# Hybrid encoder block: page names of the embedding stage, the order of the gate stage's end, the last root on ScalarE, rows stored weighted

## The chip, the cores and the metric

One core of a Trainium2 chip runs the whole program. The metric is the device time of one execution in microseconds; the time before is the median of three runs. A profiled execution, which the hardware profiler recorded, has its own time and a span, from its first to its last instruction.

## The reference

One encoder layer on 512 tokens of width 2048, all in float32:

```python
h = rms_norm(x, norm_mix_w);  proj = h @ w_in          # attention + gated linear attention
x = x + concat([y_a, y_g]) @ w_out
h = rms_norm(x, norm_ffn_w)
u = causal_depthwise_conv(h @ w_ffn_up, w_ffn_conv, b_ffn_conv)
x = x + (gelu(u_gate) * u_val) @ w_ffn_down
h = rms_norm(x, norm_ple_w)
g = sigmoid(h @ w_ple_gate)
x = x + g * (p @ w_ple_proj)
return rms_norm(x, final_norm_w)
```

The change touches the last four lines and nothing that is computed: `p @ w_ple_proj` (the embedding product), the gate `g`, its product and sum, and the last norm.

## The kernel before

Everything is held transposed: 128 channels on the partitions, 512 tokens along the row. A "unit" is a pair of channel blocks (m and m + 8), so that a unit's rows form a tile of 128 x 2 x 512 (1024 elements a partition). Large matrix products go by a Strassen-like scheme with seven products (P1 to P7) of quarter size a unit; their results are summed into four quarters: C11 and C21 hold tokens 0 to 255 (`lo`), C12 and C22 tokens 256 to 511 (`hi`), the first index is the block of the pair. Each product splits its float32 operand into a high and a low part (`wsplit`, or `last` for three products of the last pair that have tiles of their own): ScalarE copies the high part, VectorE subtracts. A product is 24 matmuls of 128x256. `prep` makes the split two products ahead, `collect` takes a product from its PSUM bank into `unit.o` (tile `u`), on ScalarE where it is a quarter's first part and on VectorE where it is added to one.

The work is a list `steps` of (unit, product). `agenda[i]` holds what is done beside step i, with a key: 0 ahead of all, 1 before the product, larger keys behind it. VectorE, ScalarE and TensorE keep this program order (`InOrder`); DMA issues do not unless they are marked with `tc.keep_in_program_order`, and a planner puts them where it sees fit on the queue of the engine that issues them (SP, ScalarE or GpSimd).

Weights come into nine pages (r0 to r8) which go round: `issue` loads the next wanted operand when a page is released, operands named L from SP, sums S from SP and GpSimd.

The embedding stage lies between the attention and the output projection. It has four units; each makes four 128x512 results by six matmuls each, which ScalarE copies in pairs into a page (tile `pp_o`) and stores from its own queue to `ppd` in memory. So eight pages are filled and stored; their names come from `PP_PAGES`. The names are those of pages that other stages use: c0 to c2 for residual rows `xs`, u0 to u3 for `unit.o`.

The gate stage (`pg`) is the last: eight units, of which the last two (u6, u7) go side by side in the order P1, P2, P6, P7, P4, P5, P3 (`HALVES`), the last fourteen steps. For units 0 to 5 `after_gate` multiplies `unit.o` by the norm's row `rb`, takes the sigmoid, multiplies by the embedding rows `ppl`, adds to the residual row `xs`, stores `xs` to `x3d` and sums its squares into `acc`. For the last pair the same is done by halves: `times_norm` (norm and sigmoid) and `add_gated` (product, sum, and the squares into a page of their own, `q`). Meanwhile `reload` brings back the rows of units 0 to 5 from `x3d` into tiles `x`, and `weigh` multiplies them by the final norm's column weights; `weigh_part` does so for the last two units.

The end, from the last four products on, is written out by hand. `sum_squares` makes the mean square on TensorE (tile `ms`), put between the matmuls of P3 for the low half and behind the last product for the high half. `root_begin` and `root_end` make the reciprocal root (tile `root`), with one Newton step: before, VectorE scales and adds, ScalarE takes the square root, VectorE the reciprocal. `finish` multiplies rows of a half by the root, a unit at a time (128x512), and stores the 256 KB piece; there are sixteen, eight low and eight high.

Of the kernel before, what the change touches and what calls it, by code (L numbers as in the profile page):

```python
# [16 lines left out]
D = 2048  # L17
# [26 lines left out]
def encoder_block(ctx: ExitStack, tc: tile.TileContext, A, out):  # L44
# [345 lines left out]
    def issue():  # L390
        kept, i = 0, 0
        while i < len(wanted):
# [11 lines left out]
            if name[0] == "L":  # L404
                nc.sync.dma_start(t, src(name))
            else:
                nc.sync.dma_start(t, src("L21"))
                nc.gpsimd.dma_start(t, src("L22" if name == "S1" else "L11"), accum_op=ALU.add)  # L408
# [283 lines left out]
    def after_gate(unit):  # L692
# [5 lines left out]
                (3, 0, lambda: nc.sync.dma_start(x3d[unit.u], xs))] + squares(unit, 2)  # L698
# [26 lines left out]
    def embedding(unit):  # L725

        hi, lo = unit.w["PP"]
        for i in range(4):
            if i % 2 == 0:
                tag = PP_PAGES[(2 * unit.u + i // 2) % 3]  # L730
# [368 lines left out]
    PP_PAGES = ("c2", "u1", "c1")  # L1099
# [94 lines left out]
    def reload(i):  # L1194
        t = xtile(("R11", "R21")[i // 2], i % 2, "x3", F32)
        for j in range(2):
            m = 2 * i + j
            if m < 6:
                x3[m] = t[:, j, :].rearrange("p (s t) -> p s t", s=2)
                nc.sync.dma_start(x3[m], x3d[m])  # L1200

    def weigh(m):
        for s in range(2):
            act.activation(x3[m][:, s, :], x3[m][:, s, :], AF.Copy, scale=nfin[:, m + 8 * s:m + 8 * s + 1])
# [14 lines left out]
    def add_gated(unit, s, c):  # L1219
        o, xs = unit.o[:, s, c], unit.xs[:, s, c]  # L1220
        vec.tensor_tensor(o, o, unit.pp[:, s, c], ALU.mult)
        vec.tensor_tensor(xs, xs, o, ALU.add)
        if unit not in sq_page:
            sq_page[unit] = spare("q").rearrange("p (s t) -> p s t", s=2)
        act.activation(sq_page[unit][:, s, c], xs, AF.Square)

    end = len(steps) - 14
    for n in range(2):
        agenda[end + 2].append((0, lambda n=n: reload(n)))
    agenda[end + 7].append((0, lambda: reload(2)))  # L1230
    for m in range(4):
        agenda[end + 5 + m].append((2, lambda m=m: weigh(m)))
# [122 lines left out]
    for i, (unit, prod) in enumerate(steps[:-4]):  # L1355
# [17 lines left out]
        if i == len(steps) - 5:  # L1373
            add_gated(units[-2], both, lo_half)
        if i - len(steps) in EARLY:
            p, op, g = EARLY[i - len(steps)]
            t = xtile(op, g, "last")
            prep(len(steps) + p, (t[:, 0, :], t[:, 1, :]))
        collect(unit, prod)
        if st.chained and st is not wo and unit.head is not None and i == base[unit] + 11:  # L1380
            norm_root()
        if st is stages[-1] and unit.last is not None:
            if prod == "P4" and unit is units[-2]:
# [18 lines left out]
    def root_begin(ms):  # L1402
        w = spare("root").rearrange("p (q t) -> p q t", q=4)
        vec.tensor_scalar(w[:, 0], ms, 1.0 / D, EPS, ALU.mult, ALU.add)
        act.activation(w[:, 1], w[:, 0], AF.Sqrt)
        return w

    def root_end(w):
        a, y, t, r = (w[:, q] for q in range(4))
        vec.reciprocal(y, y)  # L1410
# [5 lines left out]
    def finish(c, r, ms):  # L1416
        for m in ms:
            t = x3[m][:, :, c]
            vec.tensor_tensor(t, t, r[:, None, :].broadcast_to([P, 2, 256]), ALU.mult)
            (nc.sync if m % 2 else nc.scalar).dma_start(out2[m][:, :, c], t)  # L1420
# [13 lines left out]
    times_norm(u7, both, lo)  # L1434
    for s in range(2):
        vec.tensor_tensor(acc[:, lo], acc[:, lo], sq(u6, s, lo), ALU.add)
    add_gated(u7, both, lo)
    collect(u6, "P5")
    product(u7, "P5")
    times_norm(u6, 1, hi)  # L1440
    weigh_part(u6, range(2), lo)
    add_gated(u6, 1, hi)
    collect(u7, "P5")
    ms = {}
# [92 lines left out]
```

## Time and profile before

| | us |
|---|---|
| median of three runs (lowest, highest) | 2245.37 (2245.11, 2250.11) |
| profiled execution, its own time | 2245.14 |
| span of the profiled execution | 2242.8 |
| mean granted TensorE clock | 0.994 |
| gate stage's last pair, first product | starts at 2174.2 |
| last product ends | 2220.4 |
| VectorE's last row done | 2238.1 |
| embedding products | 597.7 to 626.4 |

How to read the lines: times are microseconds from the span's start; PE is TensorE's matmul, PEld its weight load, DVE VectorE, ACT ScalarE, POOL GpSimd, SP the engine that issues most DMAs. A name with q (SPq, ACTq) is that engine's queue issuing a DMA. A timeline line has start, duration, engine, source line, operation, out<-in, shapes and count; brackets hold the idle time before it and who ended it. Most lines show L64, the helper that records every operation, so the tile names tell them apart. A wait for several semaphores is put down to the one that came last.

### The profile page before, as it was taken

To read this page: it belongs to the slowest core of one execution; us is meant where nothing else is said; L and a number is where in the kernel's file an instruction comes from. 1 tells how busy PE (TensorE), PEld (TensorE's weight loads), DVE (VectorE), ACT (ScalarE), POOL (GpSimd) and SP (SyncE) were. 2 spreads that over 40 slices of the span, in tenths; PEclk is the share of its full clock that TensorE was granted. 3 is DMA by queue.
4 is the path that set the end of the run, shared out by engine and by line. 5 is a ranking of instruction groups with operands and counts; after the bars stand their busy time and mean duration, and the time that the engine had idled before them with its cause. 6 is when DMAs were issued, how large, how long until landed. Compare 5 with 4: busy or idle time off the path is not lost.

```text
span 2242.8 us, 46265 instructions
## 1 busy us (share of the span) xinstructions
PE 2196.2 (98%) x18588; PEld 2145.4 (96%) x18588; DVE 1927.1 (86%) x2636; ACT 1339.5 (60%) x2001; POOL 158.7 (7%) x196
## 2 busy tenths in 40 slices
PE   9999999999999999999999999999999999999996
PEld 7899999999889999999999999999999999999995
DVE  8476777999778888999888898889898887999997
ACT  9455565777665665555555555555564554667655
POOL 0000000000000100000000000010000100000000
PEclk9999999999999999999999999999999999999997
DMA  7476865667888987888888888888876968879994
GB/s 237 137 185 186 222 202 156 186 186 195 289 251 263 329 239 205 217 231 212 225 211 226 217 221 216 221 215 224 257 238 236 314 219 270 295 255 336 273 301 148
DMA packets 190759, 518.29 MB, mean 231 GB/s; under 512 B 20272, under 2 KB 66608, under 8 KB 190544
## 3 DMA queue, kind: packets, MB, share of 16 engines
q1 hardware_dynamic: 160272, 415.72, 54.9%
q0 software_dynamic: 25920, 93.33, 23.3%
q10 hardware_dynamic: 4352, 6.29, 0.8%
q8 instruction: 145, 2.38, 0.4%
q14 instruction: 70, 0.57, 0.1%
HBM read 441.86 MB, written 71.30 MB: 229 GB/s over the span
## 4 chain that ended last, share of the span: by engine, by line
PE 79%; DVE 10%; DMA 5%; ACT 4%; issue 2%; SPq 0%; ACTq 0%; DVEq 0%; POOLq 0%
PE accA L64 41%; PE accC L64 21%; PE accB L64 10%; DVE wsplit L64 3%; DMA l<-in_w_ple_gate 1%; DMA s<-in_w_v_a 1%; DVE u L64 1%; DVE l L64 1%; PE py L64 1%; PE ptr L64 1%; DMA ppd<-pp_o 1%; ACT wsplit L64 1%; PE psc L64 1%; PE v L243 1%; PE v L244 1%
## 5 line engine op out<-in xcount | busy, mean ns | idle before, releaser
L64 DVE TENSOR_TENSOR wsplit<-l,wsplit 128x1024 fp32r<-128x1024 f32 (+1 forms) x478 | 573.6, 1201 | 117.0 <-ACT wsplit L64 116.2
L64 ACT ACTIVATE wsplit<-l 128x1024 fp32r<-128x1024 f32 (+1 forms) x478 | 497.8, 1042 | 290.3 <-PE accC L64 121.0
L64 DVE TENSOR_TENSOR wsplit<-s,wsplit 128x1024 fp32r<-128x1024 f32 (+1 forms) x251 | 301.1, 1201 | 66.1 <-ACT wsplit L64 65.7
L64 ACT ACTIVATE wsplit<-s 128x1024 fp32r<-128x1024 f32 (+1 forms) x251 | 260.8, 1039 | 61.3 <-PE accB L64 37.4
L64 ACT ACTIVATE u<-accA 128x256 f32<-128x256 f32 x302 | 114.2, 378 | 272.3 <-PE accA L64 267.1
L64 PE MATMUL accA<-up_T,wsplit 128*128 128x256 f32 x2112 | 253.6, 276 | 0.4 <-ACT wsplit L64 0.4
L64 PEld LDWEIGHTS accA<-up_T,wsplit 128*128 128x128 f32 x2112 | 245.8, 188 | 0.7 <-ACT wsplit L64 0.6
L64 DVE SCALAR_TENSOR_TENSOR cv<-u,cw,cv 128x511 f32<-128x511 f32 (+1 forms) x176 | 131.6, 748 | 3.1
L408 POOL DMA_DIRECT2D s<-in_w_up x88 | 76.3, 867 | 764.3 <-DMA s<-in_w_up 416.4
L64 PE MATMUL accA<-up_N,wsplit 128*128 128x256 f32 x1056 | 127.1, 276 | 1.2 <-DVE wsplit L64 1.2
L64 PE MATMUL accA<-dn_T,wsplit 128*128 128x256 f32 x1056 | 126.2, 276 | 1.7 <-DVE wsplit L64 1.4
L64 PE MATMUL accC<-up_N,wsplit 128*128 128x256 f32 x1056 | 126.8, 276 | 0.9 <-DVE wsplit L64 0.9
L64 PE MATMUL accB<-up_R,wsplit 128*128 128x256 f32 x1056 | 126.9, 276 | 0.5 <-DVE wsplit L64 0.5
L64 PE MATMUL accA<-up_R,wsplit 128*128 128x256 f32 x1056 | 126.9, 276 | 0.0
L64 PE MATMUL accC<-up_R,wsplit 128*128 128x256 f32 x1056 | 126.5, 276 | 0.0
L64 PEld LDWEIGHTS accA<-dn_T,wsplit 128*128 128x128 f32 x1056 | 122.5, 188 | 2.3 <-DVE wsplit L64 1.9
L64 PEld LDWEIGHTS accA<-up_N,wsplit 128*128 128x128 f32 x1056 | 123.0, 188 | 1.6 <-DVE wsplit L64 1.6
L64 PEld LDWEIGHTS accC<-up_N,wsplit 128*128 128x128 f32 x1056 | 122.9, 188 | 1.1 <-DVE wsplit L64 1.1
L64 PEld LDWEIGHTS accB<-up_R,wsplit 128*128 128x128 f32 x1056 | 123.0, 188 | 0.7 <-DVE wsplit L64 0.7
L64 PEld LDWEIGHTS accA<-up_R,wsplit 128*128 128x128 f32 x1056 | 122.9, 188 | 0.5 <-issue 0.5
L64 PEld LDWEIGHTS accC<-up_R,wsplit 128*128 128x128 f32 x1056 | 122.8, 188 | 0.0
L64 DVE TENSOR_TENSOR l<-l,l 128x1024 f32<-128x1024 f32 (+1 forms) x86 | 102.7, 1194 | 0.0
(339 smaller groups left out, 4218.0 us busy)
## 6 DMA issues: line engine op xcount, KB each, us to landing
l<-in_w_up SPq DMA_DIRECT2D x132, 512.0 KB, 4.6
s<-in_w_up SPq DMA_DIRECT2D x88, 512.0 KB, 4.9
s<-in_w_up POOLq DMA_DIRECT2D x88, 512.0 KB, 6.4
l<-in_w_dn SPq DMA_DIRECT2D x56, 448.0 KB, 5.7
l<-in_w_blk SPq DMA_DIRECT2D x48, 512.0 KB, 5.0
s<-in_w_blk SPq DMA_DIRECT2D x32, 512.0 KB, 4.5
s<-in_w_blk POOLq DMA_DIRECT2D x32, 512.0 KB, 7.7
l<-in_w_out SPq DMA_DIRECT2D x28, 512.0 KB, 5.1
```

What stands on the lines that cost most here:

```text
L64: ins = f(*args, **kw)
L243: nc.tensor.matmul(ps[t], x[:, 0, sl], wl, start=False, stop=False)
L244: nc.tensor.matmul(ps[t], x[:, 1, sl], wh, start=False, stop=kt == KD - 1)
L408: nc.gpsimd.dma_start(t, src("L22" if name == "S1" else "L11"), accum_op=ALU.add)
```

## The change

- The last pair's weight loads of kind L are marked to keep program order on SP, and so are the reloads, which move from steps 2, 2 and 7 of the last fourteen to steps 7, 8 and 9.
- Units 0 to 5 store their rows weighted: two activations write the row times the final norm's weight into `unit.o`, one step before the store, which moves one step later and reads `unit.o`. `weigh` is gone.
- `PP_PAGES` lists eight places with five names (u2, u3, c2, u1, c1, then c2, u1, c1) instead of going round three (c2, u1, c1).
- `add_gated` is parted from its squares (`make_square`). At the end gating comes earlier and in another order, the sums of squares of the low half stand after ten matmuls of P3 rather than fifteen, the low rows 4 to 7 are finished after all high ones, and low pieces all go from SP's queue.
- The root is made by logarithm, exponential (times -0.5) and an identity on ScalarE; VectorE keeps the Newton step. Table sets are named by hand: three loads, as before.

```diff
--- before.py
+++ after.py
@@ -402,7 +402,9 @@
             t = raw_page(unit, name)[:, :n]
             src = lambda q: unit.stage.weights(unit.u, q)
             if name[0] == "L":
-                nc.sync.dma_start(t, src(name))
+                d = nc.sync.dma_start(t, src(name))
+                if unit.stage is stages[-1] and unit.last is not None:
+                    tc.keep_in_program_order(d)
             else:
                 nc.sync.dma_start(t, src("L21"))
                 nc.gpsimd.dma_start(t, src("L22" if name == "S1" else "L11"), accum_op=ALU.add)
@@ -695,7 +697,8 @@
                 (0, 2, lambda: act.activation(o, o, AF.Sigmoid)),
                 (1, 1, lambda: vec.tensor_tensor(o, o, unit.pp, ALU.mult)),
                 (2, 1, lambda: vec.tensor_tensor(xs, xs, o, ALU.add)),
-                (3, 0, lambda: nc.sync.dma_start(x3d[unit.u], xs))] + squares(unit, 2)
+                (3, 3, lambda: weighted(nfin, unit)),
+                (4, 0, lambda: nc.sync.dma_start(x3d[unit.u], o))] + squares(unit, 2)
 
     blk2 = lambda w: lambda m, q: w[m + 8 * (q[1] == "2"), int(q[2]) - 1]
     stages = [Stage("wo", list(range(8)), 8, mixd, blk2(A["w_out"]), after_norm(streams[1], h2d, nffn), "s3", "dma",
@@ -727,7 +730,7 @@
         hi, lo = unit.w["PP"]
         for i in range(4):
             if i % 2 == 0:
-                tag = PP_PAGES[(2 * unit.u + i // 2) % 3]
+                tag = PP_PAGES[2 * unit.u + i // 2]
                 o = page_pool(tag).tile([P, 1024], F32, tag=tag, name="pp_o").rearrange("p (s t) -> p s t", s=2)
             pp = psum_aux("pp")
             for k in range(2):
@@ -1096,7 +1099,7 @@
     stages[0].tail = tails
     stages[:0] = [linear, front, embed]
     wo = stages[3]
-    PP_PAGES = ("c2", "u1", "c1")
+    PP_PAGES = ("u2", "u3", "c2", "u1", "c1", "c2", "u1", "c1")
     units = [u for st in stages for u in st.units]
     steps = []
     base = {}
@@ -1197,11 +1200,7 @@
             m = 2 * i + j
             if m < 6:
                 x3[m] = t[:, j, :].rearrange("p (s t) -> p s t", s=2)
-                nc.sync.dma_start(x3[m], x3d[m])
-
-    def weigh(m):
-        for s in range(2):
-            act.activation(x3[m][:, s, :], x3[m][:, s, :], AF.Copy, scale=nfin[:, m + 8 * s:m + 8 * s + 1])
+                tc.keep_in_program_order(nc.sync.dma_start(x3[m], x3d[m]))
 
     sq_page = {}
     both = slice(0, 2)
@@ -1220,16 +1219,15 @@
         o, xs = unit.o[:, s, c], unit.xs[:, s, c]
         vec.tensor_tensor(o, o, unit.pp[:, s, c], ALU.mult)
         vec.tensor_tensor(xs, xs, o, ALU.add)
+
+    def make_square(unit, s, c):
         if unit not in sq_page:
             sq_page[unit] = spare("q").rearrange("p (s t) -> p s t", s=2)
-        act.activation(sq_page[unit][:, s, c], xs, AF.Square)
+        act.activation(sq_page[unit][:, s, c], unit.xs[:, s, c], AF.Square)
 
     end = len(steps) - 14
-    for n in range(2):
-        agenda[end + 2].append((0, lambda n=n: reload(n)))
-    agenda[end + 7].append((0, lambda: reload(2)))
-    for m in range(4):
-        agenda[end + 5 + m].append((2, lambda m=m: weigh(m)))
+    for n in range(3):
+        agenda[end + 7 + n].append((0, lambda n=n: reload(n)))
 
     def mean_square(c):
         n = (c.stop - c.start) // P
@@ -1370,17 +1368,19 @@
                 f()
         if st.chained and st is not wo:
             norm_step(i - base[st.units[0]])
-        if i == len(steps) - 5:
-            add_gated(units[-2], both, lo_half)
         if i - len(steps) in EARLY:
             p, op, g = EARLY[i - len(steps)]
             t = xtile(op, g, "last")
             prep(len(steps) + p, (t[:, 0, :], t[:, 1, :]))
+        if i == len(steps) - 5:
+            add_gated(units[-2], both, lo_half)
         collect(unit, prod)
+        if i == len(steps) - 5:
+            make_square(units[-2], both, lo_half)
         if st.chained and st is not wo and unit.head is not None and i == base[unit] + 11:
             norm_root()
         if st is stages[-1] and unit.last is not None:
-            if prod == "P4" and unit is units[-2]:
+            if prod == "P4":
                 times_norm(unit, both, lo_half)
         elif prod == unit.order[-1]:
             begin = i + 1
@@ -1401,13 +1401,13 @@
 
     def root_begin(ms):
         w = spare("root").rearrange("p (q t) -> p q t", q=4)
-        vec.tensor_scalar(w[:, 0], ms, 1.0 / D, EPS, ALU.mult, ALU.add)
-        act.activation(w[:, 1], w[:, 0], AF.Sqrt)
+        act.activation(w[:, 1], ms, AF.Ln, scale=1.0 / D, bias=epst)
+        act.activation(w[:, 1], w[:, 1], AF.Exp, scale=-0.5)
+        act.activation(w[:, 0], ms, AF.Identity, scale=1.0 / D, bias=epst)
         return w
 
     def root_end(w):
         a, y, t, r = (w[:, q] for q in range(4))
-        vec.reciprocal(y, y)
         vec.tensor_tensor(t, y, y, ALU.mult)
         vec.scalar_tensor_tensor(t, t, -0.5, a, ALU.mult, ALU.mult)
         vec.scalar_tensor_tensor(r, t, 1.5, y, ALU.add, ALU.mult)
@@ -1417,7 +1417,7 @@
         for m in ms:
             t = x3[m][:, :, c]
             vec.tensor_tensor(t, t, r[:, None, :].broadcast_to([P, 2, 256]), ALU.mult)
-            (nc.sync if m % 2 else nc.scalar).dma_start(out2[m][:, :, c], t)
+            (nc.scalar if c == hi_half and m % 2 == 0 else nc.sync).dma_start(out2[m][:, :, c], t)
 
     u6, u7 = units[-2:]
     x3[6], x3[7] = u6.xs, u7.xs
@@ -1431,47 +1431,46 @@
     lo, hi = lo_half, hi_half
     sq = lambda u, s, c: sq_page[u][:, s, c]
     product(u6, "P5")
-    times_norm(u7, both, lo)
+    add_gated(u7, both, lo)
+    make_square(u7, both, lo)
+    collect(u6, "P5")
+    times_norm(u6, 1, hi)
     for s in range(2):
         vec.tensor_tensor(acc[:, lo], acc[:, lo], sq(u6, s, lo), ALU.add)
-    add_gated(u7, both, lo)
-    collect(u6, "P5")
     product(u7, "P5")
-    times_norm(u6, 1, hi)
-    weigh_part(u6, range(2), lo)
-    add_gated(u6, 1, hi)
     collect(u7, "P5")
+    times_norm(u7, 1, hi)
+    table("natural_log_exp_and_others")
     ms = {}
-    product(u6, "P3", 15, lambda: ms.update(lo=sum_squares(lo, [acc[:, lo], sq(u7, 0, lo), sq(u7, 1, lo)])))
-    times_norm(u7, 1, hi)
-    weigh_part(u7, range(2), lo)
-    add_gated(u7, 1, hi)
+    product(u6, "P3", 10, lambda: ms.update(lo=sum_squares(lo, [acc[:, lo], sq(u7, 0, lo), sq(u7, 1, lo)])))
     w0 = root_begin(ms["lo"])
-    weigh(4)
-    weigh_part(u6, (1,), hi)
+    table("sigmoid_and_others")
+    for u in (u6, u7):
+        add_gated(u, 1, hi)
+        make_square(u, 1, hi)
+    collect(u6, "P3")
+    times_norm(u6, 0, hi)
     r0 = root_end(w0)
-    collect(u6, "P3")
     product(u7, "P3")
-    times_norm(u6, 0, hi)
+    add_gated(u6, 0, hi)
+    make_square(u6, 0, hi)
+    collect(u7, "P3")
+    times_norm(u7, 0, hi)
+    table("natural_log_exp_and_others")
     finish(lo, r0, (0,))
-    add_gated(u6, 0, hi)
-    weigh(5)
-    weigh_part(u7, (1,), hi)
-    finish(lo, r0, (1, 2))
-    collect(u7, "P3")
     m1 = sum_squares(hi, [acc[:, hi], sq(u6, 1, hi), sq(u7, 1, hi), sq(u6, 0, hi)], done=False)
-    times_norm(u7, 0, hi)
-    finish(lo, r0, (3,))
     add_gated(u7, 0, hi)
+    make_square(u7, 0, hi)
     m1 = sum_squares(hi, [sq(u7, 0, hi)], m1)
-    finish(lo, r0, (4,))
+    finish(lo, r0, (1, 2, 3))
     w1 = root_begin(m1)
-    finish(lo, r0, (5,))
+    for u in (u6, u7):
+        weigh_part(u, range(2), hi)
+    for u in (u6, u7):
+        weigh_part(u, range(2), lo)
     r1 = root_end(w1)
-    weigh_part(u6, (0,), hi)
-    weigh_part(u7, (0,), hi)
     finish(hi, r1, range(8))
-    finish(lo, r0, (6, 7))
+    finish(lo, r0, (4, 5, 6, 7))
 
 
 def _blocks(w):
```

## The prediction

> **What bounds the kernel now.** First the page's busy line, then busy time and granted clock by stretch, to see where TensorE is not fed.
>
> ```profile
> PE 2196.2 (98%) x18588; PEld 2145.4 (96%) x18588; DVE 1927.1 (86%) x2636; ACT 1339.5 (60%) x2001; POOL 158.7 (7%) x196
> ```
>
> ```profile
> 2012.00:2174.00 162.00, 157.68 (x1361) 155.16 (x1361) 148.69 (x190) 103.97 (x154) 15.73 (x19) 1.00 0.97 303
> ...
> 2207.62:2210.22 2.60, 0.00 (x1) 0.00 (x0) 2.50 (x7) 0.98 (x2) 0.00 (x0) 0.87 0.01 3
> 2210.22:2213.79 3.57, 3.57 (x16) 3.57 (x17) 2.50 (x7) 2.89 (x8) 0.00 (x0) 0.50 0.00 0
> 2213.79:2216.37 2.58, 2.58 (x9) 2.04 (x8) 0.36 (x1) 1.94 (x3) 0.00 (x0) 0.50 0.00 0
> ```
>
> The columns are the stretch, its length, busy time of PE, PEld, DVE, ACT and POOL, then the granted clock and the DMA share. TensorE bounds the body, and only a place where it stands still can be shortened. There are two: the end (2.60 us empty, then 6.15 us at half clock, then 22 us after the last product) and the embedding products at 598 to 626 us. The chain of waits and the timelines of the end say why.
>
> ```profile
> 2185.54 9.82 DMA l<-in_w_ple_gate
> ...
> 2209.84 0.34 DVE u L64
> ...
> 2217.30 1.76 DVE root L64
> ```
>
> ```profile
> 2190.53 11.50 PE L64 MATMUL accA<-pg_T,wsplit 128*128 128x256 f32 x96
> 2201.86 2.88 PE L64 MATMUL accC<-pg_N,wsplit 128*128 128x256 f32 x24
> 2204.59 3.04 PE L64 MATMUL accC<-pg_N,last 128*128 128x256 f32 x24
> ...
> 2215.79 4.58 PE L64 MATMUL accC<-pg_R,last 128*128 128x256 f32 x33
> 2220.20 0.60 PE L64 MATMUL ms<-acc,ones 128*128 128x256 f32 x2
> 2220.64 1.02 PE L64 MATMUL ms<-q,ones 128*128 128x256 f32 x4
> ```
>
> ```profile
> 2195.44 1.06 ACT L64 ACTIVATE wsplit<-l 128x1024 fp32r<-128x1024 f32 x1 [1.60 <-DMA l<-in_w_ple_gate]
> 2196.41 1.32 ACT L64 ACTIVATE x<-x,cols 128x512 f32<-128x512 f32 x2
> ...
> 2201.97 0.37 ACT L64 ACTIVATE u<-accA 128x256 f32<-128x256 f32 x1
> 2203.97 0.63 ACT L64 ACTIVATE u<-u 128x512 f32<-128x512 f32 x1 [1.62 <-DVE u L64]
> ...
> 2206.62 0.37 ACT L64 ACTIVATE u<-accA 128x256 f32<-128x256 f32 x1
> ...
> 2226.04 0.42 ACT L64 ACTIVATE q<-xs 128x256 f32<-128x256 f32 x1 [0.98 <-DVE xs L64]
> ...
> 2227.10 1.28 ACT L64 ACT_TABLE_LOAD   x1 [0.64 <-DVE x L64]
> 2228.39 0.42 ACT L64 ACTIVATE root<-root 128x256 f32<-128x256 f32 x1
> ```
>
> ```profile
> 2203.25 0.68 DVE L64 TENSOR_TENSOR u<-u,rb 128x512 f32<-128x512 f32 x1
> ...
> 2207.02 0.69 DVE L64 TENSOR_TENSOR u<-u,rb 128x512 f32<-128x512 f32 x1 [0.97 <-ACT u L64]
> ...
> 2209.75 0.41 DVE L64 TENSOR_TENSOR u<-u,accC 128x256 f32<-128x256 f32 x1
> ...
> 2227.71 0.42 DVE L64 TENSOR_SCALAR root<-ms 128x256 f32<-128x256 f32 x1 [1.10 <-PE ms L64]
> ...
> 2232.01 3.70 DVE L64 TENSOR_TENSOR x<-x,root 128x512 f32<-128x512 f32 x6
> 2235.63 2.49 DVE L64 TENSOR_TENSOR xs<-xs,root 128x512 f32<-128x512 f32 x4
> ```
>
> Read upwards: P3 of unit 6 waits for the collect at 2209.75, which stands on VectorE behind the gating of both low halves; that begins at 2203.25, after the collect at 2201.97, which ScalarE reached late because of the load that landed at 2195.36 and of weighing rows (2196.41, and again the same pair later).
>
> **The last products.** A product takes 2.72 us (2204.59 after 2201.86, 24 matmuls, 0.113 each); the four ahead of 2201.86 took 11.33 where 10.88 are due, the fourth held up by a late collect on ScalarE. So undisturbed P5 starts at 2201.45 and P3 could at 2206.9.
>
> ```profile
> 2181.60 1.90 SPq L1200 DMA_DIRECT2D x<-x3d  x4
> ```
>
> Reloads: six DMAs move from steps 2, 2 and 7 of the last fourteen to 7, 8 and 9, on SP's queue, behind the load issued at 2185.54, which they preceded (above). That load then shares the engines with less and should land before ScalarE wants it, at about 2193.8; ScalarE loses its 1.60 us wait. If it lands as now, everything below is 0.8 later. The pinned order (the last pair's loads among themselves, then the reloads) holds a later load behind one that waits for a page; they were queued in the order of their pages anyway, so I cost it at nothing, with that same 0.8 as its bound. The reloads have until the first finish, 15 us on; the last also waits for unit 5's store, now a step later and behind two activations.
>
> Weighing leaves the end (four pairs in the loop, two behind it), about 1.22 us a pair, and comes back as six pairs in the gate stage. I cost it there at nothing: ScalarE has 58 us idle in the 162 of the first stretch, and a collect has one product, 2.72 us, before its bank is written again. Uncovered it is six times 1.22, 7.3 us. A gain below nothing is excluded, since TensorE has no stall there to give back. Behind it on ScalarE stand the next collect and the next weight split; the split runs two products ahead. SP's store waits for ScalarE instead of VectorE, with weight loads behind it that are also issued a product or more ahead.
>
> With 1.6 us less waiting and 2.4 us less weighing, ScalarE collects P4 of unit 6 when TensorE is done (2198.9). VectorE then limits, with two more splits, and starts the low-half gating at 2200.3 (before 2203.25). Sigmoid 0.63 and three 128x512 steps of 0.7 follow; unit 7's first step no longer stands behind unit 6's square and the collect of 2206.62, so it starts at 2202.3 (before 2207.02). Sigmoid, two steps and the collect of P5 end at 2205.5. That is 1.4 us before TensorE needs it: the hole closes, and with it, I expect, the half clock.
>
> P3 of unit 6 starts at 2206.9 (before 2210.22). Ten matmuls, 1.13; six of the sum of squares at 0.24 (2220.20 and 2220.64, full clock) rather than 0.43, ending at 2209.5; 38 matmuls, 4.3: the last product ends at 2213.8, before 2220.37.
>
> By the Trainium skill, "TensorE: Matmul & The Clock Gate", What's actually happening, the clock falls after an idle window of about 3.4 us; here 2.60 us of hole were followed by 0.50 for 6.15 us, so the trace is harsher. By the page the hole alone would be won and the forecast be 3 us later, about 2238.5.
>
> **Roots and last rows.** Each root loses VectorE's scale-and-add (0.42), the square root and the reciprocal (1.76), and gains logarithm, exponential and identity on ScalarE, unseen here at 128x256; nearest rows are ScalarE's 0.42 at that size, both ends within 0.1. Table loads stay three, 1.28 each. Low root: sigmoid of unit 7 ends at 2208.25, load to 2209.55, three activations to 2210.8, load to 2212.1, two squares, sigmoid of unit 6 to 2213.2. Then gating, square (2214.55), collect, norm, sigmoid of unit 7 (2215.3), load (2216.6), square (2217.05), and 1.2 to the finished sum (as from 2226.46 to 2227.71): 2218.25. VectorE's 0.42 steps fit between. From the sum to the first last row took 4.3 (2227.71 to 2232.01); now logarithm, exponential and three steps, 2.35: rows begin at 2220.6, 11.4 earlier.
>
> But twelve pieces follow instead of ten, since four low ones are put last.
>
> ```profile
> GB/s 0 0 0 0 0 0 0 98 320 15 341 347 138 123 300 229 200 0 87 329 3 0 0 0 0 324 339 336 344 347 342 344 318 349 339 343 352 116 0 0
> ...
> DMA to landing us min/median/max: 2.1/2.5/3.7
> ```
>
> VectorE makes a piece in 0.61; the stores drain one (256 KB) in 0.77 at the 340 GB/s of the first row (2218 to 2243). Now ten take from 2232.7 to 2241.8 (2238.1 and 3.7), that is ten times 0.77 and 1.4, and the span ends 1.0 later. Twelve from 2221.3 with the same 1.4 and 1.0: 2232.9. The low ones all go through SP; if one queue drains slower it costs perhaps 1 us (bounds 0 and 2). The eight last weighings, 2.7 us, run beside VectorE's rows.
>
> The Trainium skill, "ScalarE: Activation LUTs", What ACT_TABLE_LOAD costs, has 1.28 us and a drain of 1.38 behind it for each switch. All three switches now lie on the path, so by that rule the end is 4.1 us later, at 2239.6. The trace shows the 1.28 and the next activation 0.01 later (2227.10, 2228.39).
>
> **Embedding pages.** Five names instead of three for eight stores.
>
> ```profile
> 604.03 10.84 DMA ppd<-pp_o
> ```
>
> ```profile
> 609.44 1.04 SPq L328 DMA_DIRECT2D wo_T<-mix_T  x2
> ```
>
> ```profile
> 611.08 1.07 ACT L64 ACTIVATE pp_o<-pp 128x512 f32<-128x512 f32 x2
> 614.94 0.37 ACTq L739 DMA_DIRECT2D ppd<-pp_o  x1
> ...
> 622.63 1.09 ACT L64 ACTIVATE pp_o<-pp 128x512 f32<-128x512 f32 x2 [1.58 <-DMA ppd<-pp_o]
> ```
>
> ```profile
> 597.73 11.07 PE L64 MATMUL pp<-ps,wsplit 128*128 128x512 f32 x48
> 611.71 7.36 PE L64 MATMUL pp<-ps,wsplit 128*128 128x512 f32 x24 [2.92 <-ACT pp_o L64]
> 620.61 5.75 PE L64 MATMUL pp<-ps,wsplit 128*128 128x512 f32 x24 [1.53 <-ACT pp_o L64]
> ```
>
> The long wait is the third store's issue: evicted by 612.15, issued at 614.94, when the second store (604.03 and 10.84) lands, though it shares no page with it. The wo_T load at 609.44 has no page in common with a store either, and SP waited for one. So this is not a page wait, and more pages do not take it away. The one page wait, 1.58 at 622.63, is the sixth store's on the third's, and in the new list these two again share a page (c2). Pages four and five are freed of a wait that no row shows. So nothing. Ends: all of it gone, the second 48 matmuls in 10.95, about the rate of the first 48, rather than in 14.65 (611.71 to 626.36), 3.7, and as much as 2 in the first products behind them, which wait for ScalarE's splits, 5.7 together; or one more wait like the third store's, 2.8, if the reordered queues bring one. I take 0, by the page list.
>
> **Sum.** 2242.8 to 2232.9 is 9.9 us. The profiled execution took 2245.14, so 2235.2; the median is 0.23 above that: 2235.5.
>
> **Rivals.**
> The embedding waits go too, because the queues order themselves otherwise: 4.5 of the 5.7, 2231.0. For it: the transfers are saturated there and any order may change. Against: the shared pages above. Chance 0.13.
> The hole before P3 stays, or its half clock does, since ScalarE is late for another reason (unit 5's weighing stands ahead of a collect at about 2188): the gain falls by 3 to 6, 2238.5 to 2241.5, centre 2240. For it: a chain of eight alternations with 1.4 us to spare. Chance 0.18.
> Slower: in the gate stage the weighing, placed before a collect, makes it later than the next write of the bank. Each of six units then loses the 1.22, and if the hole again halves the clock (15 matmuls at 0.238 instead of 0.113, 1.9) some 3 us: 18.6 against 9.9 won, 2254. It decides from 1.65 us a unit. Against: the idle 58 us. Chance 0.05.
> The change does little: output is held by the stores, which want 9.2 us for twelve pieces whatever the root does; and ScalarE or SP eat the rest. 2244. Against: they start 11 us earlier. Chance 0.05.
>
> **How the numbers follow.** The forecast, 2233.5 to 2237.5 by itself, has the other 0.59. A measurement here tells about 0.3% (6.7 us) from nothing, so the line is at 2238.6. Faster: 0.59, 0.13 and a little of the second rival, 0.76; same: 0.18; slower: 0.06. The range, 2230.0 to 2241.0, reaches over the first two rivals and leaves some 0.15 out.
>
> **What would show it.** Right: no TensorE hole between the two P5 and P3 and the clock at 1.00 there; last product ending near span end less 19; table load, logarithm and exponential within 2.4 us ahead of the last rows; twelve rows in one block; the third embedding store still issued when the second lands. Wrong: PE waits in the gate stage on ACT, a late last weight load, or eviction waits gone at 611 to 629.

## The result, and the profile after

| | before | after |
|---|---|---|
| median, eight runs each (us) | 2244.7 | 2236.88 |
| lowest, highest | 2242.53, 2250.11 | 2234.99, 2240.25 |
| span of the profiled execution | 2242.8 | 2233.0 |
| last pair's first product to the end of the span | 68.6 | 58.7 |

The ratio of the times is 0.9966, with a 95% interval of 0.9955 to 0.9976. A second set of runs of the changed kernel, beside other kernels on another occasion, gave 0.9956 (0.9944 to 0.9968). The last row of the table is the measure used below: it starts with the last pair's first product (2174.21 before, 2174.31 after), so that it leaves out whatever happened earlier. The 68.6 of before is one execution's: another kernel with the same end took 67.7 (below), so the gain in this stretch is 9.0 to 9.9.

First busy time and clock by stretch after (the columns as in the prediction). The hole and the half clock are gone; ScalarE carries 4.8 us more in the gate stage, 108.79 instead of 103.97.

```profile
2012.00:2174.00 162.00, 157.62 (x1359) 154.91 (x1358) 147.90 (x190) 108.79 (x164) 15.56 (x18) 1.00 0.96 302
...
2204.50:2207.00 2.50, 2.50 (x24) 2.50 (x23) 2.40 (x6) 1.05 (x2) 0.00 (x0) 1.00 0.01 3
2207.00:2209.50 2.50, 2.50 (x20) 2.37 (x18) 2.10 (x7) 1.26 (x2) 0.00 (x0) 1.00 0.00 0
2209.50:2214.00 4.50, 4.50 (x39) 4.47 (x38) 2.64 (x7) 4.01 (x8) 0.00 (x0) 1.00 0.02 4
```

TensorE's timeline after: P5 twice, then P3 without a gap, with the low sum after ten matmuls.

```profile
2201.51 2.88 PE L64 MATMUL accC<-pg_N,wsplit 128*128 128x256 f32 x24
2204.23 3.04 PE L64 MATMUL accC<-pg_N,last 128*128 128x256 f32 x24
2207.11 1.36 PE L64 MATMUL accC<-pg_R,last 128*128 128x256 f32 x10
2208.31 0.60 PE L64 MATMUL ms<-acc,ones 128*128 128x256 f32 x2
...
2209.42 4.90 PE L64 MATMUL accC<-pg_R,last 128*128 128x256 f32 x38
...
2217.52 0.70 PE L64 MATMUL ms<-q,ones 128*128 128x256 f32 x2 [1.48 <-ACT q L64]
```

ScalarE's timeline after: unit 5's weighing, the last weight split (no wait for the load any more, where 1.60 stood before), the collect of P4, then the table loads and the high root.

```profile
2186.74 1.33 ACT L64 ACTIVATE u<-xs,cols 128x512 f32<-128x512 f32 x2
...
2193.83 1.05 ACT L64 ACTIVATE wsplit<-l 128x1024 fp32r<-128x1024 f32 x1
...
2198.99 0.38 ACT L64 ACTIVATE u<-accA 128x256 f32<-128x256 f32 x1 [0.44 <-PE accA L64]
...
2208.66 1.28 ACT L89 ACT_TABLE_LOAD   x1
2209.95 0.47 ACT L64 ACTIVATE root<-ms,cols 128x256 f32<-128x256 f32 x1
...
2215.76 1.28 ACT L89 ACT_TABLE_LOAD   x1
2217.06 0.42 ACT L64 ACTIVATE q<-xs 128x256 f32<-128x256 f32 x1
2218.26 0.47 ACT L64 ACTIVATE root<-ms,cols 128x256 f32<-128x256 f32 x1 [0.79 <-PE ms L64]
```

VectorE's timeline after: start of the low gating (2203.25 before), collect of P5 (2209.75 before), first of the last rows (2232.01 before) and the last.

```profile
2199.92 0.69 DVE L64 TENSOR_TENSOR u<-u,rb 128x512 f32<-128x512 f32 x1
...
2205.35 0.41 DVE L64 TENSOR_TENSOR u<-u,accC 128x256 f32<-128x256 f32 x1
...
2220.66 3.70 DVE L64 TENSOR_TENSOR x<-x,root 128x512 f32<-128x512 f32 x6
...
2226.69 1.29 DVE L64 TENSOR_TENSOR xs<-xs,root 128x512 f32<-128x512 f32 x2
```

SP's queue after: the last weight load, now ahead of all six reloads.

```profile
2185.63 0.33 SPq L405 DMA_DIRECT2D l<-in_w_ple_gate  x1
2188.09 0.32 SPq L701 DMA_DIRECT2D x3d<-u  x1
2188.51 3.54 SPq L1203 DMA_DIRECT2D x<-x3d  x6
```

The embedding stage after, in the chain of waits and on ScalarE. The third store is issued at 613.17, just as the second lands (603.52 and 9.57 is 613.09); the sixth eviction still waits for a store. The order is that of before; only the transfers differ in length, so that ScalarE, done with the third eviction at 612.80, stands 0.4 us at the issue here instead of 2.8.

```profile
603.52 9.57 DMA ppd<-pp_o
```

```profile
613.17 0.37 ACTq L742 DMA_DIRECT2D ppd<-pp_o  x1
...
621.25 1.09 ACT L64 ACTIVATE pp_o<-pp 128x512 f32<-128x512 f32 x2 [2.04 <-DMA ppd<-pp_o]
```

### The profile page after: what moved, and what is told of

Read it like the earlier page. It is cut to its first block, busy times and chain, and to the rows that moved or that the text cites. A ratio compares the mean times of both kernels' runs of the same rounds, so it can differ in the third digit from the quotient of the medians.

```text
span 2233.0 us, 46278 instructions
## 1 busy us (share of the span) xinstructions
PE 2192.7 (98%) x18588; PEld 2143.9 (96%) x18588; DVE 1921.8 (86%) x2632; ACT 1339.0 (60%) x2005; POOL 158.3 (7%) x196
## 4 chain that ended last, share of the span: by engine, by line
PE 83%; DVE 8%; DMA 3%; ACT 3%; issue 2%; ACTq 0%; DVEq 0%; SPq 0%; POOL 0%; POOLq 0%
PE accA L64 43%; PE accC L64 22%; PE accB L64 10%; DVE wsplit L64 3%; PE v L244 1%; PE v L243 1%; PE v L242 1%; DMA dn_R<-g_R 1%; PE py L64 1%; PE ptr L64 1%; PE psc L64 1%; DMA ppd<-pp_o 1%; DVE u L64 1%; ACT wsplit L64 1%; DMA dn_N<-g_N 1%
```

## The experiments

"Stretch" is the time from the last pair's first product to the end of the span. Ratios are to the kernel before, with their 95% intervals.

| kernel | ratio | first product | span | stretch |
|---|---|---|---|---|
| five pages alone | 0.9996 (0.9987 to 1.0005) | 2176.49 | 2244.2 | 67.7 |
| hole filled | 1.0005 (0.9994 to 1.0015) | 2175.93 | 2243.8 | 67.9 |
| order alone | 0.9986 (0.9978 to 0.9995) | 2176.32 | 2241.3 | 65.0 |
| change, weighing at the end | 0.9980 (0.9970 to 0.9990) | 2177.54 | 2241.3 | 63.8 |
| change, old root | 0.9971 (0.9960 to 0.9982) | 2174.25 | 2236.7 | 62.5 |
| change, early reloads | 0.9958 (0.9946 to 0.9970) | 2179.54 | 2238.8 | 59.3 |
| change, three pages | 0.9958 (0.9945 to 0.9970) | 2174.69 | 2233.4 | 58.7 |
| change, stores from GpSimd | 0.9977 (0.9967 to 0.9987) | 2185.61 | 2244.3 | 58.7 |
| change, sixth page of its own | 0.9952 (0.9940 to 0.9964) | 2175.83 | 2234.5 | 58.7 |
| change, two rows earlier | 0.9956 (0.9943 to 0.9969) | 2177.40 | 2235.0 | 57.6 |
| change again | 0.9956 (0.9944 to 0.9968) | 2177.10 | 2235.8 | 58.7 |
| both last improvements | 0.9940 (0.9928 to 0.9952) | 2173.60 | 2231.1 | 57.5 |

**Are the pages worth anything?** Two kernels: the one before with the new page list, and the changed one with three pages.

```diff
-    PP_PAGES = ("c2", "u1", "c1")                       # before, taken mod 3
+    PP_PAGES = ("u2", "u3", "c2", "u1", "c1", "c2", "u1", "c1")
```

> The kernel before with the new page list alone. Theory (the long embedding wait is not a page wait): no gain, median within 2 us of before; the third store is still issued only when the second has landed, and the sixth eviction still waits for the third store's landing (some 1 to 2 us); the end of the gate stage takes as long as before (68.6 us from the last pair's first product to the end of the span). Rival (pages were the wait): 3 to 5.7 us less, and no eviction waits for a store.

> The changed kernel with the three pages of before. Theory (all comes from the end): as the changed kernel, 8 to 10 us less than before, with 58.7 us from the last pair's first product to the end. Rival (pages gave part): only 4 to 6 us less than before, with the embedding products 3 us longer than in the changed kernel.

By itself the list gives 0.9996, no change; without it the change gives 0.9958 and the same stretch of 58.7. In the kernel before with five pages, the third store is still late (evictions from 612.29, issue at 616.89), and the sixth eviction still waits:

```profile
616.89 0.37 ACTq L739 DMA_DIRECT2D ppd<-pp_o  x1
...
624.15 1.09 ACT L64 ACTIVATE pp_o<-pp 128x512 f32<-128x512 f32 x2 [1.20 <-DMA ppd<-pp_o]
```

So the theory held on both sides, and all that was won lies in the last stretch. The stretch of the first, 67.7, is 0.9 shorter than before without any change there. The half clock makes the difference. The hole ahead of P3 is as long, but the 15 matmuls behind it take 3.08 us instead of 3.57:

```profile
2212.58 3.08 PE L64 MATMUL accC<-pg_R,last 128*128 128x256 f32 x15 [2.63 <-DVE u L64]
```

By the clock records of the two traces the granted clock was 0.50 for 6.83 us before (from 2209.54, inside the hole) and for 3.41 us here (from 2213.22, behind it).

**Was it a page wait? Two further runs.** The stores from GpSimd's queue, and a page list in which the sixth result no longer follows the third in c2.

```diff
-                nc.scalar.dma_start(ppd[m % 8:m % 8 + 2, m // 8]...
+                nc.gpsimd.dma_start(ppd[m % 8:m % 8 + 2, m // 8]...
```

```diff
-    PP_PAGES = ("u2", "u3", "c2", "u1", "c1", "c2", "u1", "c1")
+    PP_PAGES = ("u2", "u3", "c2", "u1", "c1", "u2", "u3", "c2")
```

> The changed kernel with the eight embedding stores issued from GpSimd's queue instead of ScalarE's. Theory (ScalarE stands at the third store's issue until the second store has landed, an order among transfers and not a page): ScalarE no longer stands there, the second half of the embedding products begins no later and runs at the rate of the first, and from the first embedding product to the first product of the output projection it takes 25 to 26.5 us instead of 27.8; 1 to 3 us less in all. Rival (the saturated transfers or the pages hold it up either way): the wait moves to an eviction, 27 to 28.5 us, and no gain.

> The changed kernel with the embedding's sixth, seventh and eighth result in pages u2, u3 and c2, so that the sixth no longer shares a page with the third. Theory (the one page wait in the trace is the sixth eviction's, 2.04 us on ScalarE): that wait is gone, the third store's issue still waits for the second's landing, and the first product of the output projection comes 0 to 1.5 us earlier; the whole within 1.5 us of the changed kernel's. Rival (no page wait matters at all): the sixth eviction waits as long as before for a landing.

From GpSimd: ScalarE no longer stands after the third eviction (the third and fourth, two copies each, follow one another from 612.03), and GpSimd issues that store 0.3 us after its eviction. So ScalarE stood at the issue from its own queue; neither the page nor the evicted data held the store. But the stores now queue with GpSimd's weight loads, evictions wait 3.74 and 4.92 us for a store, and the first products of the output projection pay for it. My theory had the place of the wait and missed the effect, which is the rival's "the wait moves to an eviction". From the first embedding product to the first of the output projection it took 26.8 us, between the two ranges.

```profile
612.03 2.04 ACT L64 ACTIVATE pp_o<-pp 128x512 f32<-128x512 f32 x4
...
621.81 1.09 ACT L64 ACTIVATE pp_o<-pp 128x512 f32<-128x512 f32 x2 [3.74 <-DMA ppd<-pp_o]
...
631.29 1.08 ACT L64 ACTIVATE pp_o<-pp 128x512 f32<-128x512 f32 x2 [4.92 <-DMA ppd<-pp_o]
```

```profile
613.40 0.75 POOL L742 DMA_DIRECT2D ppd<-pp_o  x1 [3.56 <-ACT pp_o L64]
```

```profile
635.14 8.31 PE L64 MATMUL accB<-wo_R,wsplit 128*128 128x256 f32 x48 [4.20 <-ACT wsplit L64]
```

With a page of its own the sixth eviction waits no more for a store, while the third issue still comes at a landing:

```profile
617.52 0.37 ACTq L742 DMA_DIRECT2D ppd<-pp_o  x1
...
624.06 1.09 ACT L64 ACTIVATE pp_o<-pp 128x512 f32<-128x512 f32 x2 [0.50 <-ACT pp_o L64]
```

What that is worth is small: the ratio 0.9952 and the changed kernel's 0.9966 and 0.9956 have overlapping intervals. The two runs show that it isn't the page; what it is instead is read from the records of the traces. A transfer reports its landing by a semaphore, a counter that others can wait for. The transfers of SP and ScalarE together use eight of them, GpSimd's eight others, and in all fourteen traces no transfer of SP or ScalarE is issued before the last one on its semaphore has landed. The third store has the second's semaphore: it is issued 0.08 us after that landing in before (614.86, 614.94), and 0.07 or 0.08 after it in eleven of the thirteen kernels that store from ScalarE; in the other two its own eviction ended later. The load at 609.44 has the first store's, which landed at 609.37. From GpSimd the third store got one that had been free since 540.7, but there the second store had landed by 612.56, so that run does not test it. A kernel that hands the semaphores out otherwise was not run.

**Does closing the hole explain the end?** The kernel before, with 24 matmuls into an unused bank in the hole.

```diff
+    filled = psum_aux("fill")[:, :256]
+    for n in range(24):
+        ten.matmul(filled, u7.w["P5"][0][:, :P], u7.stage.x["N1", 0][:, 0, 0:256], start=True, stop=True)
     product(u6, "P3", 15, lambda: ...)
```

> The kernel before with 24 idle matmuls put into the 2.60 us hole ahead of P3 of the last pair; nothing else is changed. Theory (the hole costs its length and then half clock): the clock stays at 1.00 behind the hole, the 15 matmuls take 1.7 us instead of 3.57 and the sum of squares 1.45 instead of 2.58, so the low root begins some 3 us earlier and the end comes 2 to 3 us earlier. Rival (by the 3.4 us idle window of the Trainium skill's page TensorE: Matmul & The Clock Gate, a hole of 2.6 us does not lower the clock, and the 0.50 has another cause, such as the operands): the 15 matmuls still take about 3.5 us and the end is unchanged.

TensorE did what the theory said, and the end did not. Fifteen matmuls took 1.8 us (2212.26 to 2214.05) at a clock of 1.00, not 3.57 at 0.50. But the stretch is 67.9, against 68.6 before and 67.7 with five pages alone, where the hole was open; the ratio is 1.0005. The low sum is done early and VectorE takes it at 2216.01; then ScalarE has a square and a table load ahead of the square root, and VectorE waits for it. Before, the square root came 0.95 us after the end of the table load (the third fence below):

```profile
2209.38 3.04 PE L64 MATMUL fill<-pg_N,last 128*128 128x256 f32 x24
2212.26 1.96 PE L64 MATMUL accC<-pg_R,last 128*128 128x256 f32 x15
```

```profile
2216.57 1.28 ACT L64 ACT_TABLE_LOAD   x1
2217.86 0.42 ACT L64 ACTIVATE root<-root 128x256 f32<-128x256 f32 x1
```

```profile
2216.85 0.42 ACT L64 ACTIVATE root<-root 128x256 f32<-128x256 f32 x1 [0.95 <-DVE root L64]
```

```profile
2210.30:2212.50 2.20, 2.20 (x20) 2.20 (x19) 2.13 (x5) 0.66 (x2) 0.00 (x0) 1.00 0.01 4
```

```profile
2218.31 1.75 DVE L64 RECIPROCAL root<-root 128x256 f32<-128x256 f32 x1 [1.88 <-ACT root L64]
```

The last bracket is the finding: VectorE had nothing to do for 1.88 us but wait for ScalarE's root. The table load ends 41.7 to 41.9 us after the first product in all three kernels, and no root begins before it; hole and half clock cost only what they add to that, 0.95 in the execution of before and nothing with five pages alone. Removing them gains at most 0.7 us here. The theory held for TensorE and fell for the end; what sets the end is the alternation of ScalarE and VectorE. The run settles where the half clock comes from, too: with the hole filled the clock stays at 1.00, with the hole empty it was 0.50 for a while in both traces (before, and five pages alone).

**What is the new root worth?** The changed kernel with the scale-and-add, square root and reciprocal of before.

```diff
-        act.activation(w[:, 1], ms, AF.Ln, scale=1.0 / D, bias=epst)
-        act.activation(w[:, 1], w[:, 1], AF.Exp, scale=-0.5)
-        act.activation(w[:, 0], ms, AF.Identity, scale=1.0 / D, bias=epst)
+        vec.tensor_scalar(w[:, 0], ms, 1.0 / D, EPS, ALU.mult, ALU.add)
+        act.activation(w[:, 1], w[:, 0], AF.Sqrt)
...
+        vec.reciprocal(y, y)
```

> The changed kernel with the root of before (scale and add on VectorE, square root, VectorE's reciprocal) and without the two named loads of the logarithm's table. Theory (sum of steps): from the finished high sum to the first last row 4.0 to 4.3 us instead of 2.4; but the third table load no longer stands ahead of the last square, so the sum itself is up to 1.3 earlier; the end is 0.3 to 1.6 us later than the changed kernel's. Rival (the root is worth its whole 1.95 and more through VectorE's reciprocal beside the gating): 2 to 4 us later.

The stretch is 62.5, 3.75 longer, so the rival was right and the theory counted one root where there are two. The first products of the two profiles are at 2174.25 and 2174.31, so times compare directly. VectorE and ScalarE with the old root:

```profile
2212.47 1.75 DVE L64 RECIPROCAL root<-root 128x256 f32<-128x256 f32 x1
...
2224.36 3.70 DVE L64 TENSOR_TENSOR x<-x,root 128x512 f32<-128x512 f32 x6
```

```profile
2216.43 0.42 ACT L64 ACTIVATE q<-xs 128x256 f32<-128x256 f32 x1 [3.42 <-DVE xs L64]
```

The reciprocal of the low root stands on VectorE ahead of unit 6's gating, so its square comes at 2216.43 instead of 2214.54. The table load that ScalarE no longer makes ahead of the last square gives a little back; the high sum is taken at 2220.30 instead of 2218.26, 2.0 later. From there to the first last row it is 4.06 (to 2224.36) instead of 2.40 (2218.26 to 2220.66), 1.7 more. Together 3.7.

**What is the weighing worth, and the order?** First the changed kernel with rows weighed at the end again, and with it the reloads at their old steps (the marked order on SP stays).

```diff
-                (3, 3, lambda: weighted(nfin, unit)),
-                (4, 0, lambda: nc.sync.dma_start(x3d[unit.u], o))] + squares(unit, 2)
+                (3, 0, lambda: nc.sync.dma_start(x3d[unit.u], xs))] + squares(unit, 2)
...
-        agenda[end + 7 + n].append((0, lambda n=n: reload(n)))
+        agenda[end + (2, 2, 7)[n]].append((0, lambda n=n: reload(n)))
+    for m in range(4):
+        agenda[end + 5 + m].append((2, lambda m=m: weigh(m)))
...
+    weigh(4)
     table("sigmoid_and_others")
...
     w1 = root_begin(m1)
+    weigh(5)
```

> The changed kernel with the rows of units 0 to 5 stored unweighted, reloaded at steps 2, 2 and 7 as before, and weighed at the end (four pairs in the loop, two among the roots). Theory (weighing and the late weight load hold ScalarE up ahead of the low gating): the low gating begins at about 2203 instead of 2199.9, P5's collect comes after TensorE wants it, a hole of 1 to 2 us returns ahead of P3, and with the pair weighed between low root and squares the end is 2 to 4 us later than the changed kernel's. Rival (ScalarE has idle time enough there as well): within 0.5 us of the changed kernel.

The stretch is 63.8, 5.1 longer, more than either theory had. The first product is at 2177.54 here; VectorE's start of the low gating is 29.3 behind it, in the changed kernel 25.6 (2199.92 after 2174.31). These 3.7 come from ScalarE: a wait for the last weight load, and weighings between splits. TensorE's hole is back at 1.56, and the ten matmuls behind it take 1.46 instead of 1.36. Of the 3.7 the low root sees 3.3 (its first activation comes 39.0 us after the first product instead of 35.6). The fifth weighing pair, between the low root and its table load, adds 1.2, and the last two matmuls of the high sum 0.5: behind a gap of 1.82 us they take 1.22 at a clock of 0.50 instead of 0.70. Together 5.0 of the 5.1.

```profile
2199.05 1.06 ACT L64 ACTIVATE wsplit<-l 128x1024 fp32r<-128x1024 f32 x1 [1.88 <-DMA l<-in_w_ple_gate]
2200.01 1.32 ACT L64 ACTIVATE x<-x,cols 128x512 f32<-128x512 f32 x2
```

```profile
2206.84 0.68 DVE L64 TENSOR_TENSOR u<-u,rb 128x512 f32<-128x512 f32 x1
```

```profile
2212.75 1.46 PE L64 MATMUL accC<-pg_R,last 128*128 128x256 f32 x10 [1.56 <-DVE u L64]
...
2225.29 1.22 PE L64 MATMUL ms<-q,ones 128*128 128x256 f32 x2 [1.82 <-ACT q L64]
```

How much of that is the load? The changed kernel with weighed stores, the reloads early and no pinned order:

```diff
-                if unit.stage is stages[-1] and unit.last is not None:
-                    tc.keep_in_program_order(d)
...
-                tc.keep_in_program_order(nc.sync.dma_start(x3[m], x3d[m]))
+                nc.sync.dma_start(x3[m], x3d[m])
...
-        agenda[end + 7 + n].append((0, lambda n=n: reload(n)))
+        agenda[end + (2, 2, 9)[n]].append((0, lambda n=n: reload(n)))
```

> The changed kernel with the first four reloads at step 2 of the last fourteen, as before, and no marked order on SP. Theory: the last weight load lands at about 2195 again (9 us instead of 5) and the low gating begins 0.8 us later, but the 1.4 us to spare ahead of P3 take that up: the end within 0.5 us of the changed kernel's. Rival (the pinned order is what closes the hole): 1.5 us or more later, with a hole ahead of P3.

The stretch is 59.3, 0.6 longer; the theory had up to 0.5. ScalarE waits for the load again, the low gating begins 0.9 later, and TensorE has no hole: the slack of 1.4 us before P3 takes that up. What is left comes by the low root, 0.5 later. The last two matmuls stand behind the same gap of 1.82 as in the run above, here at full clock.

```profile
2200.43 1.06 ACT L64 ACTIVATE wsplit<-l 128x1024 fp32r<-128x1024 f32 x1 [1.26 <-DMA l<-in_w_ple_gate]
```

```profile
2223.29 0.70 PE L64 MATMUL ms<-q,ones 128*128 128x256 f32 x2 [1.82 <-ACT q L64]
```

Then the new order alone: the old root, rows weighed at the end, reloads early and nothing pinned (the edits of the three runs above together).

> The changed kernel with the old root, weighing at the end, early reloads and no marked order: only the order of the end (and the pages) is left of the change. The old root has cost 3 to 3.7 us of the 9.9. Theory (the parts add up: root 3 to 4, weighing and reloads 2 to 4, order the rest): 2 to 4 us less than before. Rival (the order is worth most by itself): 6 us or more less than before.

The stretch is 65.0, 3.6 less than before's 68.6 (2.7 less than the 67.7 with five pages alone), in the range expected. With the changed kernel and two of the runs above this makes a square, all in the new order. It is not a pure one: the upper row has the early reloads too, which alone cost 0.6, and of its two kernels only the right one keeps the marked order.

| stretch | old root | new root |
|---|---|---|
| rows weighed at the end | 65.0 | 63.8 |
| rows stored weighted | 62.5 | 58.7 |

The parts do not add up. The root is worth 1.2 with the weighing at the end and 3.75 without; the weighing, with its reloads, 2.5 with the old root and 5.1 with the new. They stand on two engines of one chain: while ScalarE weighs its pair behind the low root, VectorE's reciprocal costs nothing. VectorE's gating of unit 6 behind the low root comes 43.7 us after the first product with the old root (2220.03 less 2176.32) and 43.9 with the new (2221.39 less 2177.54), so of the root only the high one counts there.

```profile
2220.03 0.42 DVE L64 TENSOR_TENSOR u<-u,ppl 128x256 f32<-128x256 f32 x1
```

```profile
2221.39 0.43 DVE L64 TENSOR_TENSOR u<-u,ppl 128x256 f32<-128x256 f32 x1 [1.84 <-ACT u L64]
```

**Are the stores the last bound?** The changed kernel with two low rows finished ahead of the high root.

```diff
-    finish(lo, r0, (1, 2, 3))
+    finish(lo, r0, (1, 2, 3, 4, 5))
...
-    finish(lo, r0, (4, 5, 6, 7))
+    finish(lo, r0, (6, 7))
```

> The changed kernel with low rows 4 and 5 finished ahead of the high root, so that ten pieces instead of twelve follow it. Theory (the last stores drain at 0.77 us a piece and set the end): VectorE, 0.7 us idle there, begins the last rows 0.5 us later, two pieces less are to drain, 1.5, so the end is some 1 us earlier than the changed kernel's. Rival (VectorE's rows set the end, 0.61 each): the two rows only change places and the end is the same, within 0.3 us.

The stretch is 57.6, 1.1 shorter. Six low rows (0 to 5) now stand ahead of the root, so the last rows begin 46.7 us after the first product (2224.14 less 2177.40) instead of 46.3. Two pieces less at 0.77 are 1.5, less that 0.4: 1.1. Were VectorE's rows the bound, at 0.61 a row, the same count would give 0.8; and the time from VectorE's last row to the end, which then would not change, is 5.0 us with twelve pieces and 4.7 with ten, in before too. The transfers of the changed kernel (2218 to 2233, in 40 slices) say the same: from about 2222.5 on they run at some 340 GB/s, 0.77 us a piece, to the end.

```profile
GB/s 123 317 366 330 344 350 268 0 0 0 0 137 328 361 330 336 352 333 355 331 350 339 341 339 344 344 347 333 344 336 344 344 341 350 344 341 47 0 0 0
```

```profile
2224.14 3.70 DVE L64 TENSOR_TENSOR x<-x,root 128x512 f32<-128x512 f32 x6
```

**Both small gains together, and the change once more.** Two rows earlier with the sixth result on a page of its own; beside it the changed kernel itself.

> The changed kernel with low rows 4 and 5 ahead of the high root and with pages u2, u3, c2 for the embedding's last three results. Theory (the parts add): from the last pair's first product to the end 57.6 us instead of 58.7, the embedding up to 0.5 us shorter, the whole 1 to 2 us less than the changed kernel. Rival (the stretch ahead of the gate stage varies by more than that from run to run): no difference from the changed kernel that the intervals resolve.

> The changed kernel once more, beside the last one on the same chip. If the end is what was won, its last stretch is again 58.7 us within 0.3, wherever the last pair begins; the median 7 to 10 us less than before. If the end varied, the stretch would vary with the time.

The first has a median of 2233.14 us, ratio 0.9940 (0.9928 to 0.9952), and is the best version run here; the changed kernel had 2236.0, 0.9956 (0.9944 to 0.9968). The stretch is 57.5 against 58.7, which repeats the gain of two rows earlier. That its time is below the changed kernel's is likely but not settled, since the intervals overlap. From the first embedding product to the output projection's fifth product (its first with `wo_N`) it was 41.1 us, against 42.4 beside it and 41.3 in the first profile after: no more than two executions of one kernel differ by.

## Why the prediction was right

- **The forecast.** 2235.5 against a measured 2236.9, a span of 2232.9 against 2233.0. That the spans agree within 0.1 is in part luck: the profiled execution was the shortest of its set (2234.99), its last pair began where before's did, and before's half clock was the longer of the two seen. By medians the gain is 7.8, where the forecast had 9.9; by stretches it is 9.0 to 9.9. The stretch is 58.7 in all four kernels that differ from the changed one only in the embedding stage or not at all; where the last pair begins is what moved (2173.6 to 2179.5 over all kernels of the table but the one with stores from GpSimd).
- **Reloads.** The last weight load is issued ahead of all six (before, four of them preceded it, not six), and ScalarE's 1.60 wait is gone, as said. The price of the other case was given as 0.8; it measured 0.6.
- **The chain to P3.** Low gating from 2200.3 by the sum, 2199.92 measured; collect of P5 done at 2205.5, measured 2205.76 (2205.35 and 0.41); P3 from 2206.9, measured 2207.11; clock at 1.00.
- **The clock.** The prediction set the trace against the Trainium skill, "TensorE: Matmul & The Clock Gate", What's actually happening, which has the clock fall after an idle window of about 3.4 us. The runs side with the trace: 0.50 after holes of 2.60 and 2.63 us, 1.00 with the hole filled and behind a hole of 1.56.
- **Roots.** The low root's first activation at 2209.95 (2209.55 by the sum), the last square ending at 2217.48 (2217.05), the high sum taken at 2218.26 (2218.25), the last rows from 2220.66 (2220.6). The drain of 1.38 behind a table load, of the Trainium skill, "ScalarE: Activation LUTs", What ACT_TABLE_LOAD costs, is not in the trace: 2208.66 and 1.28 end at 2209.94 and the logarithm starts at 2209.95; the high one likewise (2215.76, 2217.06). One sign was written wrong: the last table load stands 4.9 us ahead of the last rows, as the sum itself had it (load to 2216.6, rows at 2220.6), and not within 2.4; logarithm and exponential do.
- **Weighing in the gate stage at nothing.** ScalarE took the 4.8 us more there, and TensorE's busy time in that stretch is the same, 157.62 against 157.68. No run moved the weighing alone.
- **Pages at nothing.** Shown from both sides, and the reason too: the third store waits for the second's landing whatever page it uses, c1 with three pages or c2 with five; by the records of the traces the two share a semaphore.
- **Twelve pieces at 0.77.** Shown by the two rows moved and by the rate at the end. The last low pieces went through SP alone at that rate; the 1 us that the prediction named for a slower single queue did not appear.

What was misjudged lies beside the sum. The prediction named the hole and the half clock first among what could be won at the end; filling the hole of before gained at most 0.7. The sum was right because it did not count them, but followed ScalarE and VectorE step by step. The second rival's 3 to 6 us for a late ScalarE are not refuted by that: where ScalarE was late in the new order (weighing at the end), the hole was back and the stretch 5.1 longer, but by the late chain and not by the hole. And the old root and the weighing are each worth more inside the change (3.75 and 5.1) than was expected of them before their runs (0.3 to 1.6, 2 to 4): the first because both roots stand on the path, the second because the pair behind the low root and the gap at the high sum come on top of the late gating.

## What to carry to other kernels

At the end of a kernel follow the two engines that hand work to each other, instruction by instruction, and count a hole of TensorE only if that chain passes through it. Before adding buffers, look at what the late transfer lands behind: if it shares no buffer with the one that it waits for, more buffers do nothing; look whether it shares a semaphore. Price parts of a change against the final version as well as alone, and measure the stretch that they touch, since what happens earlier moves by more than they are worth.

## What the runs showed of the hardware

By the clock records of all fourteen traces every stretch of one granted clock that ends within the program is a whole multiple of 3.41 us long, wherever TensorE's gaps lie. The length of a gap alone did not decide: gaps of 2.60 and 2.63 us, ahead of P3 in before and with five pages alone, went with a clock of 0.50 for 6.83 and 3.41 us; a gap of 1.82 was followed by 0.50 in one kernel (two matmuls in 1.22 us) and by 1.00 in another (0.70 us), and gaps of 1.54 and 1.56 ahead of P3 by 1.00. Stores of 256 KB left at 0.77 us each (some 340 GB/s) when they followed each other. Stores put on GpSimd's queue stood behind its weight loads, and evictions waited 3.7 and 4.9 us for them. An activation followed a table load of 1.28 us 0.01 us later. The start of the last pair differed by 3 us between two executions of the same kernel (2174.31 and 2177.10), all of it ahead of the change's last stretch.
